# Five pairs of split-weight buffers moved to ten different distances from the stationary tiles in one layer of a hybrid attention / state-space trunk

## The chip, the core and the metric

The kernel runs on one core of one Trainium2 chip. The metric is the device time of one execution in microseconds (us). Start-to-start times of single matmuls are given in nanoseconds (ns).

## What is computed

One layer of a trunk with three groups of heads beside each other, in float32, for 256 tokens of width 4096:

```python
def hybrid_layer(x, norm_w, w_in, w_out, ...):
    h = rms_norm(x, norm_w)
    proj = jnp.einsum('bsd,de->bse', h, w_in)          # 256 x 4096 by 4096 x 14392
    ...                                                # three groups of heads, their gates and norms
    mix = jnp.concatenate([o_fox, o_ssd, o_gdn], axis=-1)
    return x + jnp.einsum('bse,ed->bsd', mix, w_out)   # 256 x 4096 by 4096 x 4096
```

The groups are a forgetting attention (fox), a Mamba-2 scan (ssd) and a gated delta rule (gdn). Nearly all arithmetic lies in the two projections.

## The kernel before

Both projections are worked off in panels of 512 output columns: 28 panels of `w_in` (and 56 gate columns apart), then 8 panels of `w_out`. A panel runs over 32 tiles of the inner dimension (KT = 32). The stationary operand is the activation: for each tile k a buffer `xhl{k}` (later, in the same place, `mhl{k}`) of 128 partitions x 2 x 256 fp32r numbers, the high part and the low part of the same values, 2048 bytes a partition. The moving operand is the weight. SyncE loads two tiles at a time into a buffer `wr` (L226); `split_w` then makes the high part `wh` with a cast on ScalarE (L203) and the low part `wl` with a subtraction on VectorE (L204), each 128 x 512 fp32r, 2048 bytes a partition. `product` issues six matmuls of 512 columns for the tile, for each of the two blocks of 128 tokens (tb):

```python
nc.tensor.matmul(ps[tb], h, wh, start=k == 0, stop=False)           # L214
nc.tensor.matmul(ps[tb], lo, wh, start=False, stop=False)           # L215
nc.tensor.matmul(ps[tb], h, wl, start=False, stop=k == KT - 1)      # L216
```

So `wh` is read four times, `wl` twice, and each matmul has a weight load of its own, of 128 columns of `xhl` (512 bytes a partition).

The pool `wstream` holds four buffers of `wr` and five each of `wh` and `wl`, used in turn. Pools lie in memory in the order in which they are opened. In the built program every `xhl` starts at an address that leaves 128 when divided by 512 (the first at 16512), and so does every half of one, of 512 bytes; the `wh` stand at 98432, 100480, 102528, 104576, 106624 and the `wl` at 108672 to 116864, all of which leave 128 as well. The distance between what a matmul streams and what the next one's weight load reads is thus 0 modulo 512 in all 6,912 of them (36 panels x 32 x 6). The pools behind `wstream` (constants, heads, small tiles) begin at 118912; the heads' tiles leave 32.

The heads' work is cut into generators that `drive` advances by a step after each tile, so that it is strewn between the panels' matmuls. The order of all instructions is set when the program is built. Two more places have matmuls of 512 columns: `gate_chunk` (L243) streams `xhl{k}` past eight stationary tiles of 112 columns, `gw`, which stand 448 bytes apart from a place that leaves 32, and `warm_up` (L154) runs eleven matmuls of zeros at the start.

Of the kernel before, what the change touches and what calls it, by code (L numbers as in the profile page):

```python
# [11 lines left out]
F32R = mybir.dt.float32r  # L12
# [7 lines left out]
P = 128  # L20
# [37 lines left out]
CONV.update({f"sx{_u}": 512 * _u for _u in range(3)}, sB=1536, sC=2048)  # L58
TAPS = 4

C_GN = 0
C_FQ = C_GN + 1
C_FK = C_FQ + 1
# [27 lines left out]
@with_exitstack  # L91
def tile_hybrid(ctx: ExitStack, tc: tile.TileContext, x, xT, w, wo, prm, cst, lev, cvw, out):
    nc = tc.nc

    xp = ctx.enter_context(tc.tile_pool(name="xsplit", bufs=1))
    wp = ctx.enter_context(tc.tile_pool(name="wstream", bufs=5))
    cp = ctx.enter_context(tc.tile_pool(name="const", bufs=1))
    hp = ctx.enter_context(tc.tile_pool(name="heads", bufs=1))
    sp = ctx.enter_context(tc.tile_pool(name="small", bufs=4))
# [98 lines left out]

    def split_w(wr, pinned=False):

        wh = wp.tile([P, 512], F32R, tag="wh", name="wh")
        wl = wp.tile([P, 512], F32R, tag="wl", name="wl")
        a = nc.scalar.copy(wh, wr)  # L203
        b = nc.vector.tensor_tensor(out=wl, in0=wr, in1=wh.bitcast(F32), op=ALU.subtract)  # L204
        if pinned:
            pin(a)
            pin(b)
        return wh, wl
# [12 lines left out]
    def panel(src, lhs):  # L221

        ps = [pp.tile([P, 512], F32, tag="proj", name="proj") for _ in range(2)]
        for c in range(0, KT, CK):
            wr = w_tile()
            nc.sync.dma_start(out=wr, in_=src[:, c:c + CK, :])  # L226
            for j in range(CK):
                wh, wl = split_w(wr[:, j, :])
                product(ps, lhs(c + j), wh, wl, c + j)
                drive()  # L230
        return ps
# [28 lines left out]
    def first_panels(srcs):  # L260
# [24 lines left out]
        for k in range(KT):  # L285
            c, j = k // CK * CK, k % CK
            if j == 0 and 0 < c < KT - CK:
                load(c + CK)
            if k == 8:
                load_consts(xhl[k][:, 0, 0:1].bitcast(F32))  # L290
                clear_past(xhl[k][:, 0, 0:1].bitcast(F32))
            for i in range(len(srcs)):
                wh, wl = split_w(wr[c, i][:, j, :], True)
                product(ps[i], xhl[k], wh, wl, k)
            if k + 1 < KT:
                t, jj, n = xr[k + 1]
                split_x(t, jj, k + 1)
            t, jj, n = xr[k]
            if jj == n - 1:
                square_x(t, n)  # L300
            if (k + 1) % GK_STEP == 0:
                gate_chunk(gp, k + 1 - GK_STEP)
# [195 lines left out]
    def to_mix(src, kt0, ncol, step=0):  # L498

        n = src[0].shape[1]  # L500
        for i0 in range(0, n, 2):
            m = min(2, n - i0)
            ps = bank("mps")
            for i in range(m):
                for tb in range(2):
                    nc.tensor.transpose(ps[:, i * T + tb * P:i * T + tb * P + P], src[tb][:, i0 + i, :], ident)  # L506
            for i in range(m):
                kt = kt0 + i0 + i
                if kt < 12:
                    mt = cp.tile([P, T], F32, name=f"mix{kt}")  # L510
                elif kt < 24:
                    mt = h1([P, T], F32, name=f"mix{kt}")
                else:
                    if kt % 4 == 0:
                        st["fmix"] = r4([P, 4, T], name=f"fmix{kt}", tag="keep")
                    mt = st["fmix"][:, kt % 4, :]
                c = ncol + step * (i0 + i)
                nc.scalar.activation(mt, ps[:, i * T:(i + 1) * T], AF.Copy, scale=prm_s[:, c:c + 1])
                mix[kt] = mt
            yield  # L520

    def gated_norm(ot, c, z):

        for tb in range(2):
            for h in range(HG):
                nc.vector.scalar_tensor_tensor(out=ot[tb][:, h, :], in0=ot[tb][:, h, :],
                                               scalar=c[:, tb * HG + h:tb * HG + h + 1],
                                               in1=z[:, tb, h * P:h * P + P], op0=ALU.mult, op1=ALU.mult)
            yield 2
# [205 lines left out]
    def gdn_out(g, z):  # L735
        yield from gated_norm(gd[g]["ot"], gd[g]["c"], z)
        yield from to_mix(gd[g]["ot"], 4 * g, C_GN)

# [280 lines left out]
    for i in range(8):  # L1019
        cs = slice(i * 512, (i + 1) * 512)  # L1020
        ps = panel(wo[i].rearrange("p (j n) -> p j n", n=512), mix_split)
        for tb in range(2):
# [3 lines left out]
            n = 2 if i == 7 and tb == 1 else 1  # L1026
# [39 lines left out]
def _trace(nc, arrays):  # L1066
    args = {n: nc.dram_tensor(f"in_{n}", v.shape, mybir.dt.from_np(v.dtype), kind="ExternalInput").ap()
            for n, v in arrays.items()}
    args["out"] = nc.dram_tensor("out_0", (T, D), F32, kind="ExternalOutput").ap()
    with tile.TileContext(nc, schedule_with_timeline_sim=True) as tc:  # L1070
        tile_hybrid(tc, **args)
# [11 lines left out]
```

## Time and profile before

| | us |
|---|---|
| median of 2 runs | 1742.24 (1742.17 to 1742.31) |
| the profiled execution | 1739.72 |
| its span, from the first to the last instruction | 1737.9 |
| TensorE busy (matmuls) | 1715.7, 99% |
| weight loads (beside the matmuls) | 1410.1, 81% |
| VectorE busy | 1162.0, 67% |
| ScalarE busy | 933.0, 54% |
| mean granted TensorE clock | 0.999 |

A matmul's own duration is no measure of its cost here: matmuls are pipelined, one of 512 columns is shown with 0.39 us, and the next starts after 0.23 us. What a matmul costs is read from one start to the next. The timeline gives starts to 0.01 us, so that a single step is known to some 10 ns only; over a row of steps the mean is sharper. Where a row stands for several matmuls, its start is that of the first.

### The profile page before, as it was taken

The numbers are of one execution on the slowest core, as the hardware profiler recorded it, in microseconds if no ns is written. First come the engines' busy times: TensorE is split into PE (matmuls) and PEld (weight loads), VectorE is DVE, ScalarE is ACT, GpSimd is POOL, SyncE is SP. The second block draws the span as 40 slices with busy tenths as digits, with TensorE's granted clock in tenths as the row PEclk, the third lists the DMA queues.
The fourth block names the chain that finished last, engine by engine and source line by source line (L and its number), as shares of the span: only waits on it lengthen the run. The fifth ranks groups of instructions, "written<-read, shape, count | busy, mean of one in ns | idle before, by whom it ended". The sixth has DMA issues, their size and how long they took to land.

```text
span 1737.9 us, 24143 instructions
## 1 busy us (share of the span) xinstructions
PE 1715.7 (99%) x8165; PEld 1410.1 (81%) x8165; DVE 1162.0 (67%) x2121; ACT 933.0 (54%) x1635; POOL 89.1 (5%) x73
## 2 busy tenths in 40 slices
PE   9999999998999999999999999999999999999999
PEld 7888878786888778887788888888888888888887
DVE  7668777786676887768776665555755765555554
ACT  6665555445555464546555555556555754444443
POOL 0000020001000020000222100000000000000000
PEclk9999999999999999999999999999999999999999
DMA  8768876665665857667886666665666677777764
GB/s 292 225 216 286 266 233 204 220 200 173 212 224 154 277 163 224 205 199 264 262 274 196 183 186 185 191 202 172 184 194 183 180 243 216 218 217 217 206 205 139
DMA packets 119507, 368.86 MB, mean 212 GB/s; under 512 B 12629, under 2 KB 16045, under 8 KB 119383
## 3 DMA queue, kind: packets, MB, share of 16 engines
q1 hardware_dynamic: 114055, 358.15, 66.4%
q10 hardware_dynamic: 5328, 9.17, 1.5%
q8 instruction: 64, 1.05, 0.2%
q14 instruction: 60, 0.49, 0.1%
HBM read 355.61 MB, written 11.67 MB: 211 GB/s over the span
## 4 chain that ended last, share of the span: by engine, by line
PE 72%; DMA 2%; DVE 1%; issue 1%; ACT 1%; SPq 0%; DVEq 0%; ACTq 0%
PE proj L216 22%; PE proj L214 22%; PE proj L215 22%; DMA tap<-in_cvw 1%; PE yp L809 1%; DVE wl L204 0%; PE kkps L603 0%; PE mps L506 0%; PE zps L581 0%; PE yps L581 0%; PE zqs L581 0%; DMA dmat<-gsum 0%; PE cor L581 0%; ACT L432 0%; PE o L581 0%
## 5 line engine op out<-in xcount | busy, mean ns | idle before, releaser
L204 DVE TENSOR_TENSOR wl<-wr,wh 128x512 fp32r<-128x512 f32 x1152 | 799.0, 708 | 476.9 <-ACT wh L203 420.6
L203 ACT CAST wh<-wr 128x512 fp32r<-128x512 f32 x1152 | 704.8, 621 | 713.8 <-DVE wl L204 304.0
L214 PE MATMUL proj<-wh,xhl 128*128 128x512 f32 x1792 | 707.0, 395 | 9.0 <-ACT wh L203 6.0
L215 PE MATMUL proj<-wh,xhl 128*128 128x512 f32 x1792 | 702.9, 392 | 0.0
L216 PE MATMUL proj<-wl,xhl 128*128 128x512 f32 x1792 | 678.8, 396 | 6.3 <-DVE wl L204 6.0
L214 PEld LDWEIGHTS proj<-wh,xhl 128*128 128x128 f32 x1792 | 337.3, 188 | 81.0 <-ACT wh L203 8.4
L216 PEld LDWEIGHTS proj<-wl,xhl 128*128 128x128 f32 x1792 | 334.9, 188 | 82.2 <-DVE wl L204 14.8
L215 PEld LDWEIGHTS proj<-wh,xhl 128*128 128x128 f32 x1792 | 337.3, 188 | 69.1
L215 PE MATMUL proj<-wh,mhl 128*128 128x512 f32 x512 | 199.4, 390 | 0.0
L214 PE MATMUL proj<-wh,mhl 128*128 128x512 f32 x512 | 199.3, 390 | 0.0
L216 PE MATMUL proj<-wl,mhl 128*128 128x512 f32 x512 | 195.5, 390 | 0.0
L216 PEld LDWEIGHTS proj<-wl,mhl 128*128 128x128 f32 x512 | 96.2, 188 | 19.9
L214 PEld LDWEIGHTS proj<-wh,mhl 128*128 128x128 f32 x512 | 96.1, 188 | 19.9
L215 PEld LDWEIGHTS proj<-wh,mhl 128*128 128x128 f32 x512 | 96.2, 188 | 19.9
L473 DVE TENSOR_TENSOR shift<-shift,tap 128x1024 f32<-128x1024 f32 x42 | 51.3, 1221 | 20.5 <-DMA tap<-in_cvw 20.3
L648 DVE TENSOR_TENSOR tn<-tn,zps 128x512 f16<-128x512 f16 (+1 forms) x36 | 24.5, 682 | 3.5 <-PE zps L581 3.5
L649 DVE TENSOR_TENSOR tt<-tt,zqs 128x512 f16<-128x512 f16 (+1 forms) x36 | 24.5, 680 | 0.0
L793 POOL TENSOR_TENSOR xd<-xtok,spl 128x384 f32<-128x384 f32 (+2 forms) x12 | 16.7, 1398 | 127.5 <-ACT xtok L485 78.2
L430 DVE TENSOR_SCALAR dmat<-dmat,csum 128x128 f32<-128x128 f32 x72 | 16.4, 287 | 9.8 <-DMA dmat<-gsum 9.8
L657 POOL TENSOR_TENSOR res<-cst_s,tn 128x512 f32<-128x512 f32 x6 | 8.2, 1360 | 265.1 <-DVE tn L648 253.4
L639 ACT CAST y<-yps 128x512 f16<-128x512 f32 x36 | 19.3, 586 | 3.9 <-PE yps L581 3.8
L432 ACT ACTIVATE dmat<-dmat 128x384 f32<-128x384 f32 (+1 forms) x22 | 12.2, 554 | 14.5 <-DVE dmat L430 14.3
(302 smaller groups left out, 918.7 us busy)
## 6 DMA issues: line engine op xcount, KB each, us to landing
wr<-in_w SPq DMA_DIRECT2D x446, 512.0 KB, 3.8
wr<-in_wo SPq DMA_DIRECT2D x128, 512.0 KB, 3.6
shift<-past SPq DMA_DIRECT2D x42, 512.0 KB, 5.1
tap<-in_cvw SPq DMA_DIRECT2D x61, 256.0 KB, 6.4
xres<-in_x ACTq DMA_DIRECT2D x16, 256.0 KB, 4.9
xr<-in_xT SPq DMA_DIRECT2D x15, 257.0 KB, 4.9
out<-xres ACTq DMA_DIRECT2D x15, 256.0 KB, 4.2
dmat<-gsum SPq DMA_DIRECT2D x16, 192.0 KB, 6.5
```

The costliest lines, as they stand in the source:

```text
L203: a = nc.scalar.copy(wh, wr)
L204: b = nc.vector.tensor_tensor(out=wl, in0=wr, in1=wh.bitcast(F32), op=ALU.subtract)
L214: nc.tensor.matmul(ps[tb], h, wh, start=k == 0, stop=False)
L215: nc.tensor.matmul(ps[tb], lo, wh, start=False, stop=False)
L216: nc.tensor.matmul(ps[tb], h, wl, start=False, stop=k == KT - 1)
L430: pin(nc.vector.tensor_scalar(out=t[:, i, :], in0=t[:, i, :], scalar1=st["cs"][:, tb, c0 + i:c0 + i + 1], scalar2=0.0, op0=ALU.subtract, o ...
L473: pin(nc.vector.tensor_tensor(out=sh, in0=sh, in1=wj, op=ALU.mult))
L639: nc.scalar.copy(y[tb], v4(ps))
L648: nc.vector.tensor_tensor(out=tn2, in0=tn[tb], in1=v4(zp), op=ALU.subtract)
L649: nc.vector.tensor_tensor(out=tt2, in0=tt[tb], in1=v4(zq), op=ALU.subtract)
L793: nc.gpsimd.tensor_tensor(out=xd[:, o:o + n, :], in0=xv, in1=bc(st["spl"][:, tb, h0:h0 + n], 64), op=ALU.mult)
L809: nc.tensor.matmul(yp[:, h * 64:h * 64 + 64], m[h // 3][:, h % 3, :], xd[:, h, :], start=True, stop=True)
```

## The change

The five turns of `wh` and `wl` become ten buffers with tags of their own, each with a small tail that is never used: 16 elements (64 bytes), or 8 (32 bytes) for `wl3`. The names and the shape that the rest of the kernel sees are as before.

```diff
+SHIFT = {"wh": (4, 4, 4, 4, 4), "wl": (4, 4, 4, 2, 4)}
...
-    wp = ctx.enter_context(tc.tile_pool(name="wstream", bufs=5))
+    wp = ctx.enter_context(tc.tile_pool(name="wstream", bufs=1))
+    turn = [0]
...
     def split_w(wr, pinned=False):
 
-        wh = wp.tile([P, 512], F32R, tag="wh", name="wh")
-        wl = wp.tile([P, 512], F32R, tag="wl", name="wl")
+        i = turn[0]
+        turn[0] = (i + 1) % 5
+        wh, wl = (wp.tile([P, 512 + 4 * SHIFT[n][i]], F32R, tag=f"{n}{i}", name=f"{n}{i}_")[:, 0:512]
+                  for n in ("wh", "wl"))
```

In the built program the buffers now alternate, and their distances from the stationary tiles modulo 512 are:

| turn | 0 | 1 | 2 | 3 | 4 |
|---|---|---|---|---|---|
| wh: address, distance | 98432, 0 | 102656, 128 | 106880, 256 | 111104, 384 | 115296, 480 |
| wl: address, distance | 100544, 64 | 104768, 192 | 108992, 320 | 113216, 448 | 117408, 32 |

All that stands behind the pool moves up by 608 bytes; the heads' tiles then leave 128 modulo 512. No instruction is added, removed or moved: on all five engines the same operations on the same operands stand in the same order, with a wait at the same places, as the two built programs show row by row.

## Rows read from the trace of the kernel before

**Rows 1.** The page: busy time, share, instructions; the granted clock in 40 slices.

```profile
PE 1715.7 (99%) x8165; PEld 1410.1 (81%) x8165; DVE 1162.0 (67%) x2121; ACT 933.0 (54%) x1635; POOL 89.1 (5%) x73
PEclk9999999999999999999999999999999999999999
```

**Rows 2.** The page, costliest groups: busy us, mean ns of one | idle before, its releaser.

```profile
L204 DVE TENSOR_TENSOR wl<-wr,wh 128x512 fp32r<-128x512 f32 x1152 | 799.0, 708 | 476.9 <-ACT wh L203 420.6
L203 ACT CAST wh<-wr 128x512 fp32r<-128x512 f32 x1152 | 704.8, 621 | 713.8 <-DVE wl L204 304.0
L214 PE MATMUL proj<-wh,xhl 128*128 128x512 f32 x1792 | 707.0, 395 | 9.0 <-ACT wh L203 6.0
L214 PEld LDWEIGHTS proj<-wh,xhl 128*128 128x128 f32 x1792 | 337.3, 188 | 81.0 <-ACT wh L203 8.4
L214 PE MATMUL proj<-wh,mhl 128*128 128x512 f32 x512 | 199.3, 390 | 0.0
```

**Rows 3.** Waits of PE: who waited for whom, us in total, times, longest.

```profile
PE proj L216 <- DVE wl L204: 6.0, 12, 1.1
PE proj L214 <- ACT wh L203: 6.0, 2, 4.2
PE proj L214 <- ACT raw_gz L992: 3.0, 2, 2.2
```

**Rows 4.** Groups of PE from 1500 to 1700 us, the output projection.

```profile
L214 PE MATMUL proj<-wh,mhl 128*128 128x512 f32 x295 | 114.9, 389 | 0.0
L215 PE MATMUL proj<-wh,mhl 128*128 128x512 f32 x294 | 114.5, 389 | 0.0
L216 PE MATMUL proj<-wl,mhl 128*128 128x512 f32 x295 | 112.3, 389 | 0.0
```

**Rows 5.** Timeline of PE and PEld, 403 us: start us, us, engine, line, operation.

```profile
402.94 0.40 PE L216 MATMUL proj<-wl,xhl 128*128 128x512 f32 x1
402.94 0.19 PEld L214 LDWEIGHTS proj<-wh,xhl 128*128 128x128 f32 x1
```

**Rows 6.** Timeline of PE, 26.6 to 28.9 us: a chunk of gate columns.

```profile
26.60 0.39 PE L216 MATMUL proj<-wl,xhl 128*128 128x512 f32 x1
26.83 2.02 PE L243 MATMUL gproj<-xhl,gw 128*112 128x512 f32 x8
28.68 0.40 PE L214 MATMUL proj<-wh,xhl 128*128 128x512 f32 x1
```

**Rows 7.** Timeline of PE, 884 to 888 us: behind two matmuls of a head.

```profile
884.10 0.81 PE L827 MATMUL yops<-sst,sC 128*128 128x384 f32 x2
...
884.98 0.39 PE L215 MATMUL proj<-wh,xhl 128*128 128x512 f32 x1
885.21 0.40 PE L216 MATMUL proj<-wl,xhl 128*128 128x512 f32 x1
...
885.68 0.39 PE L215 MATMUL proj<-wh,xhl 128*128 128x512 f32 x1
885.90 0.39 PE L216 MATMUL proj<-wl,xhl 128*128 128x512 f32 x1
...
887.06 0.39 PE L215 MATMUL proj<-wh,xhl 128*128 128x512 f32 x1
```

**Rows 8.** Timeline of PE, 640 to 651 us: two blocks of head matmuls.

```profile
639.77 0.39 PE L214 MATMUL proj<-wh,xhl 128*128 128x512 f32 x1
...
644.08 0.62 PE L581 MATMUL yps<-tn,mb 128*128 128x128 f16 x8
...
644.83 0.40 PE L216 MATMUL proj<-wl,xhl 128*128 128x512 f32 x1
...
646.90 0.39 PE L216 MATMUL proj<-wl,xhl 128*128 128x512 f32 x1
...
649.40 0.40 PE L581 MATMUL zps<-y,tt 128*128 128x128 f16 x4
649.63 0.39 PE L581 MATMUL zqs<-tt,y 128*128 128x128 f16 x4
649.86 0.39 PE L581 MATMUL zps<-y,tt 128*128 128x128 f16 x4
650.08 0.39 PE L581 MATMUL zqs<-tt,y 128*128 128x128 f16 x4
```

## The prediction

> **What bounds the kernel now.** I read the page first, then PE's waits, then the timeline, because only starts tell what a matmul costs here. [...] The two engines that feed TensorE are busy for two thirds and for half of the time, and each idles longest for the other or for free buffers [rows 1, 2]; PE waits for them for some 15 us in all [rows 3]. So the span is the number of matmuls times the distance from one start to the next, and all that the change can do must show in that distance.
>
> The distance in the undisturbed state: from 1500 to 1700 us, 884 matmuls touch the window [rows 4]. A matmul of 0.39 us touches it when it starts between 1499.61 and 1700, so 200.39 us / 884 = 226.7 ns. The same comes out in the input projection: 19 steps from 639.77 to 644.08 us, 226.8 ns [rows 8]. [...] The step is also the same for `wh` and `wl`, for `xhl` and `mhl`.
>
> Beside each matmul runs the weight load of the next, from the same start on [rows 5], for 188 ns [rows 2]. Both read the state buffer, and in this kernel always at places that are equal modulo 512 bytes.
>
> **What the change touches.** It adds no instruction, takes none away and moves none. The casts and subtractions have the same shapes (621 and 708 ns [rows 2]); they write to starts that are multiples of 32 bytes as before, and I cost them at nothing: their engines idle 714 and 477 us in those groups [rows 2], so a rise of a tenth in 799.0 + 704.8 us of work would stay hidden; without that cover, were PE to wait for each, a tenth of 708 ns x 1,152 would be 82 us. The rotation is still five deep. What is left is one thing: in 6,912 matmuls the place of the moving operand against the place of the weight load beside it changes, from always 0 to ten values, four matmuls at one, two at the next, and so on. At one turn in five `wh` stays at 0, though between others.
>
> **What a step costs at other distances.** The trace of before holds no panel matmul at another distance in a steady run, so I bound it from rows near by.
>
> - The gate columns are the nearest: the same 512 moving columns of fp32r, with eight stationary tiles 448 bytes apart, so that the distance changes with every matmul (the loads that run beside them lie at 160, 224, 288, 352, 416, 480, 32 and, for the panel's matmul behind, 0). From 26.83 to 28.68 us are eight steps: 231.3 ns [rows 6]. The load has 112 columns in place of 128. The step just before, in which the distance went from 0 to 96, took 0.23 us, no more than the others.
> - Out of step at distance 0: behind two head matmuls the panel's steps are not 226.7 at once. From 884.98 to 887.06 are nine steps, 231.1 ns in the mean [rows 7]; the two from 885.21 to 885.68 take 235 ns each, the next, to 885.90, 0.22 us. Behind a block of fp16 matmuls it is the same: 644.83 to 646.90, nine steps, 230.0 ns [rows 8]. After nine or ten steps the row is back at 226.7. So the short step is a state into which a row of matmuls settles when nothing disturbs it, and a disturbance costs some 4 ns a step until then.
>
> With the change something is disturbed after every second or fourth matmul: the moving operand's place jumps by 64 bytes, or by 32 at two places of the round. A row that needs nine undisturbed steps to settle gets four at most. I therefore take the unsettled step for all of them, 231.1 ns, between the gate rows' 231.3 and the 230.0 behind fp16 blocks: 231.1 - 226.7 = 4.4 ns more.
>
> **How many pay it.** Some are unsettled now. 8,165 - 6,912 = 1,253 matmuls are not the panels'; in the rows they come in blocks of 2, 8 and 16 [rows 7, 8], 8.7 in the mean, which makes 144 blocks and, with nine steps each, 1,300 unsettled steps; some blocks lie closer than nine steps, so I take 1,200. The sum: (6,912 - 1,200) x 4.4 ns = 25.1 us. On the profiled execution's 1739.72 us (span 1737.9 and 1.8 around it) that gives 1764.8; the runs' median is 2.5 us above that execution, so 1767 for a median, and I say 1766. The waits of [rows 3] may shrink by a few us as TensorE becomes slower, which is why I go down and not up.
>
> **Bounds of the step.** Above: 235 ns, the two dear steps of [rows 7], for all that settle now: 8.3 x 5,712 = 47 us, 1790; for all 6,912, 57 us, 1799. Below: 0.22 us, the short step of [rows 7], some 3 ns below the settled one: 6,912 x 3 = 21 us less, 1721. I stay at 231.1 since two independent kinds of rows give it as a mean, while both ends are single steps that follow one another.
>
> [...] In the trace the gate rows, whose loads wander, are at 231.3 where the panels are at 226.7 [rows 4, 6]. [...]
>
> **Rivals.**
>
> 1. *The place does not matter; nothing happens.* What unsettles a row would be the block of other matmuls, and in the gate columns the shorter load. For it: the first step at distance 96 is as short as the others [rows 6]. Against: the gate rows do not settle over eight steps. Time: 1742.
> [...]
> 3. *The bad distances last.* If a wrong distance holds a row at the dear step rather than at the mean of a swing, the steps are 235: 1790, over 2% more. For it: such steps stand next to each other in [rows 7]. Against: they are followed by a short one.
>
> **How the numbers follow.** The forecast, steps of 229.5 to 233 ns, 1756 to 1778: 0.55. Rival 1: 0.17. Rival 2: 0.13. Rival 3, 1778 to 1799: 0.15. The range for 8 in 10 takes in rival 1, most of rival 3 and a part of rival 2: 1732 to 1796; the forecast's own is 1756 to 1778. 2% of the time is 35 us, about what a measurement of this kernel can tell from no change: 1707 and 1777. Faster by more needs more than half of the distances free: 0.05. Slower by more is rival 3 and the upper edge of the forecast: 0.22. Within 2%: 0.73.
>
> **What would show it.** If right: the window from 1500 to 1700 us, now 884 matmuls, holds 867 or so; the steps vary from buffer to buffer and do not settle to 226.7 anywhere, also where no head works; the casts, subtractions and waits are as before. Wrong, by rival 1: 884 again. [...] By rival 3: about 853, with steps of 235 that come back with the same buffer. Were the casts or subtractions to take longer, or PE's waits in [rows 3] to grow, the cause would lie outside all of this.

## The result, and the profile after

| | before | after |
|---|---|---|
| median, us | 1742.24 | 1764.71 (1763.06 to 1766.37, 2 runs) |
| profiled execution, us | 1739.72 | 1766.37 |
| ratio, 95% interval | | 1.0135 (1.0109 to 1.0162) |

The changed kernel is slower by 1.35% (the two medians alone make 1.29%), less than 2% and clear of the noise. The forecast was 1766.

The page of the changed kernel, its busy times and its clock, which answer to [rows 1]:

```profile
PE 1743.2 (99%) x8165; PEld 1409.9 (80%) x8165; DVE 1162.8 (66%) x2121; ACT 932.5 (53%) x1635; POOL 86.5 (5%) x73
PEclk9999999999999999999999999999999999999999
```

The counts are the same on every engine, VectorE and ScalarE worked as long as before (1162.8 against 1162.0, 932.5 against 933.0 us), and the clock is the full one. Only the matmuls take 27.5 us longer. PE's idle time is 1764.6 - 1743.2 = 21.4 us of the span, against 22.2 before. So nothing waits more; the matmuls follow each other more slowly.

How much more slowly, from the windows of the changed kernel (busy us and instructions of each engine, granted clock, DMA), where the same stretch held 884 matmuls before [rows 4]:

```profile
1500.00:1700.00 200.00, 200.00 (x864) 161.96 (x863) 104.52 (x156) 89.72 (x147) 0.00 (x0) 1.00 0.70 210
```

200.39 us / 864 = 231.9 ns a step, where it was 226.7. No head works in this stretch, so that the row has all the time to settle, and does not. The timeline of the same stretch, PE alone:

```profile
1600.12 0.39 PE L220 MATMUL proj<-wh__15166,mhl 128*128 128x512 f32 x1
1600.35 0.39 PE L221 MATMUL proj<-wl__15167,mhl 128*128 128x512 f32 x1
1600.59 0.39 PE L219 MATMUL proj<-wh__15176,mhl 128*128 128x512 f32 x1
1600.81 0.40 PE L220 MATMUL proj<-wh__15176,mhl 128*128 128x512 f32 x1
1601.05 0.39 PE L221 MATMUL proj<-wl__15177,mhl 128*128 128x512 f32 x1
...
1603.60 0.39 PE L220 MATMUL proj<-wh__15198,mhl 128*128 128x512 f32 x1
1603.83 0.39 PE L221 MATMUL proj<-wl__15199,mhl 128*128 128x512 f32 x1
```

16 steps from 1600.12 to 1603.83 us, 231.9 ns again. The order on PE is also seen here: two matmuls with `wh`, one with `wl`, two, one. The moving operand's place therefore changes after every second and every single matmul, more often than the four and two that the prediction spoke of.

Taken over the whole trace, the 6,534 steps under 260 ns from one panel matmul to the next have a mean of 231.6 ns (before: 227.5); the difference makes 6,534 x 4.1 = 27 us, which is the whole loss of the profiled execution (26.7). Sorted by the buffer that is streamed, the steps to the next start in the output projection run from 229.0 ns at 192 to 234.5 at 64, with 230.8 at 256 and 232.0 at 0. Even the turn at distance 0, whose place is that of before, takes 232.0.

### The profile page after: what moved, and what is told of

Its sections match the earlier page's. It is cut to its first block, busy times and chain, and to the rows that moved or that the text cites. A ratio compares the mean times of both kernels' runs of the same rounds, so it can differ in the third digit from the quotient of the medians.

```text
span 1764.6 us, 24143 instructions
## 1 busy us (share of the span) xinstructions
PE 1743.2 (99%) x8165; PEld 1409.9 (80%) x8165; DVE 1162.8 (66%) x2121; ACT 932.5 (53%) x1635; POOL 86.5 (5%) x73
## 4 chain that ended last, share of the span: by engine, by line
PE 69%; DMA 3%; DVE 2%; issue 1%; ACT 1%; SPq 0%; DVEq 0%; ACTq 0%
PE proj L221 22%; PE proj L219 21%; PE proj L220 21%; DMA tap<-in_cvw 2%; DMA dmat<-gsum 1%; DMA wr<-in_w 1%; PE yp L814 0%; PE kkps L608 0%; PE mps L511 0%; PE zps L586 0%; PE yps L586 0%; PE zqs L586 0%; PE cor L586 0%; DVE raw_sx L479 0%; DVE shift L478 0%
## 5 line engine op out<-in xcount | busy, mean ns | idle before, releaser
L176 DVE SCALAR_TENSOR_TENSOR xhl<-xr,xhl 128x256 fp32r<-128x256 f32 x32 | 15.3, 479 | 3.5 <-ACT xhl L175 3.5
L175 ACT ACTIVATE xhl<-xr 128x256 fp32r<-128x256 f32 x32 | 16.2, 507 | 2.1 <-DMA xr<-in_xT 2.1
L631 DVE TENSOR_TENSOR mb<-m,lev_s 128x512 f16<-128x512 f16 x42 | 16.0, 416 | 0.0
L586 PE MATMUL zps<-y,tt 128*128 128x128 f16 x144 | 14.1, 220 | 1.8 <-ACT y L644 1.8
L586 PEld LDWEIGHTS <-mb 128*128 128x128 f16 x168 | 9.5, 98 | 7.9 <-issue 4.4
L574 POOL TENSOR_TENSOR ktail<-raw_gk,dec 128x512 f32<-128x512 f32 x3 | 3.5, 1168 | 228.9 <-DVE sqn L719 228.9
L586 PEld LDWEIGHTS <-tt 128*128 128x128 f16 x144 | 8.9, 98 | 7.1 <-issue 7.1
L1034 DVE TENSOR_TENSOR xres<-xres,proj 128x512 f32<-128x512 f32 (+1 forms) x17 | 10.4, 650 | 5.4 <-PE proj L221 5.4
L586 PE MATMUL zqs<-tt,y 128*128 128x128 f16 x144 | 13.9, 219 | 0.0
L814 PEld LDWEIGHTS yp<-xd,dmat 128*128 128x128 f32 x96 | 12.7, 191 | 1.1
L814 PE MATMUL yp<-xd,dmat 128*128 128x64 f32 x96 | 12.1, 267 | 0.0
```

The source lines that it names most:

```text
L175: pin(nc.scalar.activation(t[:, 0, :], xr[:, jj, 0:T], AF.Copy, scale=sc))
L586: nc.tensor.matmul(ps[:, h * P:h * P + P], lhs(h), rhs(h), start=True, stop=True)
L814: nc.tensor.matmul(yp[:, h * 64:h * 64 + 64], m[h // 3][:, h % 3, :], xd[:, h, :], start=True, stop=True)
```

## Experiments

Two theories were to be told apart. *Changing costs*: any constant distance settles at 226.7 ns, and only jumps unsettle the row (the prediction's step). *The value costs*: each distance has a step of its own, and 0 happens to be a cheap one. Where a kernel holds one distance through a panel, its buffers are 640 columns wide and a slice of 512 is taken at the wanted place; the mean step of a panel of the output projection is the time from its first to its last start divided by 191. The first of these panels still has matmuls of a head in it; there only its uninterrupted stretches count, from the tenth step on. Runs without a number of executions were executed once. Where an edit starts from the kernel of another run, it is said; `...` in an edit marks lines left out.

### Ten buffers, all at distance 0

```diff
-SHIFT = {"wh": (4, 4, 4, 4, 4), "wl": (4, 4, 4, 2, 4)}
+SHIFT = {"wh": (32, 32, 32, 32, 32), "wl": (32, 32, 32, 32, 32)}
...
```

> The changed kernel with tails of 512 bytes on all ten buffers, so that every distance is 0 again; tags, rotation and the shift of all that stands behind stay of the changed kernel's kind. If the distances are the cause, whether by their values or by their changing: steps of 226.7 ns in the output projection and 1742 us, within 3. If it is something else in the change (ten tags, other addresses of the heads' tiles): about 1764 us, steps of 231 to 232 ns.

Measured: 1738.31 us (10 runs) beside 1737.94 of the kernel before on the same chip, ratio 0.9995 (0.9981 to 1.0009). The windows of this kernel show the 884 of before:

```profile
1500.00:1700.00 200.00, 200.00 (x884) 165.69 (x883) 106.33 (x157) 90.99 (x148) 0.00 (x0) 1.00 0.68 211
```

The tags and the code of the rotation cost nothing. What stands behind the pool moves here by 5,120 bytes, a multiple of 512, and not by 608 as in the change; that its place modulo 512 is not the cause is seen from the output projection of the changed kernel, where no head works and the step is 231.9 ns all the same. It is the distances.

### One distance through a whole panel

```diff
...
-        wh = wp.tile([P, 512], F32R, tag="wh", name="wh")
-        wl = wp.tile([P, 512], F32R, tag="wl", name="wl")
+        dh, dl = place()      # by panel: 0, 64, 128, ... in the output projection
+        wh = wp.tile([P, 640], F32R, tag="wh", name="wh")[:, dh // 4:dh // 4 + 512]
+        wl = wp.tile([P, 640], F32R, tag="wl", name="wl")[:, dl // 4:dl // 4 + 512]
```

> Both buffers at one distance through a whole panel (192 matmuls), another one in the next: 0, 64, 128, 192, 256, 320, 384, 448 in the eight panels of the output projection, 26 further values in the input projection. If a change of distance unsettles a row and any constant distance settles: 226.7 ns a step in every panel after some ten matmuls, 43.5 us a panel of the output projection, 1742 to 1745 us in all. If each distance has a step of its own and 0 is a cheap one: 226.7 ns at 0 alone, 229 to 235 at the others (44.0 to 45.1 us a panel), 1764 to 1790 us. [...]

Measured: 1765.11 us, as much as the changed kernel, with a single change of distance per panel. The timeline of this kernel, the first and the last matmul of six panels (distances 64, 128, 192, 256, 320, 384):

```profile
1448.97 0.40 PE L225 MATMUL proj<-wh,mhl 128*128 128x512 f32 x1
...
1492.70 0.39 PE L227 MATMUL proj<-wl,mhl 128*128 128x512 f32 x1
1492.93 0.40 PE L225 MATMUL proj<-wh,mhl 128*128 128x512 f32 x1
...
1537.32 0.40 PE L227 MATMUL proj<-wl,mhl 128*128 128x512 f32 x1
1537.56 0.40 PE L225 MATMUL proj<-wh,mhl 128*128 128x512 f32 x1
...
1582.13 0.39 PE L227 MATMUL proj<-wl,mhl 128*128 128x512 f32 x1
1582.36 0.39 PE L225 MATMUL proj<-wh,mhl 128*128 128x512 f32 x1
...
1625.67 0.39 PE L227 MATMUL proj<-wl,mhl 128*128 128x512 f32 x1
1625.90 0.40 PE L225 MATMUL proj<-wh,mhl 128*128 128x512 f32 x1
...
1669.63 0.39 PE L227 MATMUL proj<-wl,mhl 128*128 128x512 f32 x1
1669.86 0.40 PE L225 MATMUL proj<-wh,mhl 128*128 128x512 f32 x1
...
1714.26 0.40 PE L227 MATMUL proj<-wl,mhl 128*128 128x512 f32 x1
```

| distance | 0 | 64 | 128 | 192 | 256 | 320 | 384 | 448 |
|---|---|---|---|---|---|---|---|---|
| step, ns | 226.7 | 229.0 | 232.4 | 233.4 | 226.8 | 229.0 | 232.4 | 233.4 |

For 64: (1492.70 - 1448.97) / 191 = 229.0 ns. A constant distance need not settle at 226.7. It settles, but into a short cycle of steps: 226, 229 or 230, 231 or 232 at 64; 233, 233, 234 at 192. And what counts repeats after 256 bytes, not 512: 64 and 320, 128 and 384, 192 and 448 agree to 0.1 ns. That falls to *the value costs*.

The two other distances of the change stand in the input projection of the same run, at 32 and at 480:

```profile
130.06 0.40 PE L225 MATMUL proj<-wh,xhl 128*128 128x512 f32 x1
...
134.49 0.39 PE L226 MATMUL proj<-wh,xhl 128*128 128x512 f32 x1
...
465.23 0.40 PE L225 MATMUL proj<-wh,xhl 128*128 128x512 f32 x1
...
470.13 0.40 PE L226 MATMUL proj<-wh,xhl 128*128 128x512 f32 x1
```

19 steps of 233.2 ns and 21 of 233.3.

The distance alone does not fix the cycle, however. The panel at 496 has one break, eight matmuls of a head:

```profile
1308.55 0.39 PE L225 MATMUL proj<-wh,xhl 128*128 128x512 f32 x1
...
1325.55 0.40 PE L225 MATMUL proj<-wh,xhl 128*128 128x512 f32 x1
1325.79 1.04 PE L904 MATMUL fps<-cst_s,raw_fk 128*128 128x128 f32 x8
...
1326.89 0.40 PE L227 MATMUL proj<-wl,xhl 128*128 128x512 f32 x1
...
1353.87 0.40 PE L227 MATMUL proj<-wl,xhl 128*128 128x512 f32 x1
```

75 steps of 226.7 ns ahead of it, 114 of 236.7 behind it, at the same distance. So a distance can hold a row in more than one cycle, and a disturbance can take it from one to another. What picks the cycle was not tested.

### The low part alone

Against the kernel with one distance a panel:

```diff
         p = cur["p"]
-        d = 0 if p < 0 else INNER[p] if p < 26 else OUTER[p - 26]
-        return d, d
+        return 0, (0 if p < 0 else INNER[p] if p < 26 else OUTER[p - 26])
```

> wh stays at distance 0, wl alone is moved, by another amount in each panel (0, 64, 128, ... 448 in the output projection), so that two matmuls at 0 and one at the other distance follow each other. If changing is what costs: all steps dear, 230 to 232 ns in the mean in every panel but the one at 0, about 1764 us. If the value costs: a third of the steps dear, 228.3 ns in the mean, about 1751 us.

Measured: 1758.61 us, between the two. Windows of this kernel, inside the panels with `wl` at 64, 128, 256 and 384:

```profile
1445.00:1485.00 40.00, 40.00 (x174) 32.37 (x174) 19.71 (x29) 18.02 (x30) 0.00 (x0) 1.00 0.68 217
1489.00:1529.00 40.00, 40.00 (x174) 32.27 (x173) 19.58 (x30) 17.70 (x29) 0.00 (x0) 1.00 0.68 218
1578.00:1618.00 40.00, 40.00 (x178) 33.10 (x177) 19.94 (x30) 18.40 (x30) 0.00 (x0) 1.00 0.68 220
1666.00:1706.00 40.00, 40.00 (x175) 32.50 (x174) 20.09 (x30) 18.09 (x30) 0.00 (x0) 1.00 0.65 207
```

174 matmuls in 40.39 us are some 232 ns, 178 are 227. With `wl` at 64 the panel's mean is 231.8 ns, far over (2 x 226.7 + 229.0) / 3 = 227.5, which the values alone would give, and over the step of either distance; at 256 it is 226.9, although the place changes as often. So a change inside a tile costs too, here 4.3 ns a step, but not one by 256. The agreement of distances 256 apart does not hold throughout: with `wl` at 128 the panel's mean is 232.7 ns, at 384 231.1.

### A change after every n tiles

Against the kernel with one distance a panel:

```diff
+EVERY = (8, 4, 1, 2, 4, 8, 16, 0)
...
-        p = cur["p"]
-        d = 0 if p < 0 else INNER[p] if p < 26 else OUTER[p - 26]
+        p, k = cur["p"], cur["k"]
+        cur["k"] = k + 1
+        d = 0 if p < 0 or EVERY[p % 8] == 0 else 64 * (k // EVERY[p % 8]) % 512
         return d, d
```

> Both buffers at one distance that moves by 64 bytes after every n tiles (6 n matmuls); the panels of the output projection have n = 1, 2, 4, 8, 16, never, 8, 4. If a change unsettles some nine steps at 231 ns and the row then settles at 226.7: 231, 230, 228.3, 227.5, 227.1, 226.7, 227.5, 228.3 ns in the mean of these panels. If the value costs: about the same 230 to 233 ns for every n, and 226.7 in the panel without change alone.

Measured: 1754.27 us. Panels of the output projection, against the mean of the constant steps of the same distances (230.4 ns for all eight, as for 0 to 192; 227.8 for 0 and 64):

| n | 1 | 2 | 4 | 8 | 16 | never |
|---|---|---|---|---|---|---|
| step, ns | 231.6 | 231.4 | 230.8 | 230.5 | 228.0 | 226.9 |
| by the values | 230.4 | 230.4 | 230.4 | 230.4 | 227.8 | 226.7 |

Windows of this kernel inside the panels with n = 2, 8 and 16:

```profile
1442.00:1482.00 40.00, 40.00 (x175) 32.47 (x174) 20.05 (x30) 18.41 (x30) 0.00 (x0) 1.00 0.65 212
1530.00:1570.00 40.00, 40.00 (x176) 32.59 (x175) 19.72 (x30) 17.87 (x30) 0.00 (x0) 1.00 0.68 221
1574.00:1614.00 40.00, 40.00 (x177) 32.98 (x176) 19.94 (x30) 18.17 (x30) 0.00 (x0) 1.00 0.68 221
```

Most of what lies over 226.7 is the values; what comes on top shrinks with n, from 1.2 ns at n = 1 to 0.1 at n = 8, some 5 to 12 ns for each change (6 x 1.2, 12 x 1.0, 24 x 0.4, 48 x 0.1). These changes come between tiles, by 64 bytes and for both buffers at once; the changed kernel also changes inside each tile, as the low part alone does. Neither theory alone gives this row: at n = 8 changing alone would be 227.5, and the values alone know no n.

### The stationary tiles moved instead

```diff
+    gp0 = ctx.enter_context(tc.tile_pool(name="gap0", bufs=1))
+    gp0.tile([P, 16], F32, name="gap0")
     xp = ctx.enter_context(tc.tile_pool(name="xsplit", bufs=1))
+    gp1 = ctx.enter_context(tc.tile_pool(name="gap1", bufs=1))
+    gp1.tile([P, 112], F32, name="gap1")
```

> wh and wl stay where they were (they leave 128 modulo 512), the stationary tiles move up by 64 bytes instead, so that the distance is -64, that is 448, in all 6,912 matmuls. If the distance between the two counts: the step of 448 in the run with one distance a panel, 233.4 ns in a cycle of 233, 233, 234; 6.7 ns more on some 6,540 steps, 1738 + 44 = 1782 us. If the place of the moving buffers by itself counts: 226.7 ns, 1738 us. If only a changing distance costs: 226.7 ns and 1738 us as well.

Measured: 1772.36 us (4 runs), ratio 1.0196 (1.0179 to 1.0213). The windows of this kernel:

```profile
1500.00:1700.00 200.00, 200.00 (x859) 161.15 (x858) 102.58 (x153) 87.81 (x143) 0.00 (x0) 1.00 0.66 209
```

200.39 / 859 = 233.3 ns, the step of distance 448, with the moving buffers where they always were; the run with one distance a panel had moved those and left the stationary tiles. It is the distance between the two operands and not the place of one of them, and a distance that never changes is enough for a loss of 33.5 us. The 44 that were expected counted from 226.7 ns; from the mean of before, 227.5, the sum is 6,540 x 5.8 = 38; some of it came back in the gaps over 260 ns between panel matmuls, which fell from 88.3 to 83.4 us.

### More distances

The kernel with one distance a panel, other numbers in its lists.

> One distance a panel as before, 34 others: 60, 124, 188, 248, 12, 104, 120, 200 in the output projection, multiples of 4 up to 244 in the input projection. If the step is a matter of where the moving stream meets the weight load within 256 bytes: 226 to 237 ns, each value near its neighbours (60 near 229, 124 near 232, 188 near 233, 248 between 236 and 227), none under 226.7, about 1764 us. [...]

Measured: 1769.35 us; no panel under 226.7 ns. As short as 0 are 28, 60 and 156 (226.7 each); 12 has 228.9, 124 and 188 have 230.0, 200 has 233.3, 120 has 234.3, 244 has 239.8 and 116 has 240.0. Neighbours are not alike: 120 lies 4 bytes from either of 116 and 124. Over both runs with one distance a panel 57 of the 64 multiples of 4 modulo 256 were held; 226.7 ns was the step at 0, 28, 60, 156 and 252, and in part of a panel at 240 (the 496 above). A second value at one distance is seen here too: the panel at 196 has 240.0 ns ahead of its head matmuls and 233.3 behind them. At 116 the steps are all equal, in the timeline of this kernel:

```profile
742.22 0.40 PE L225 MATMUL proj<-wh,xhl 128*128 128x512 f32 x1
...
744.86 0.40 PE L227 MATMUL proj<-wl,xhl 128*128 128x512 f32 x1
```

11 steps, 240.0 ns each.

### High and low part woven together

The loads of `xhl` and `mhl` now read every second element: one of 128 columns spans 1024 bytes in place of 512 and takes some 194 ns (33.34 us of loads in 40 us, at a step of 233.3 ns, in the first window below), where it took 188 [rows 2].

Against the kernel with one distance a panel:

```diff
-        return xp.tile([P, 2, T], F32R, tag=f"xhl{k}", name=f"{name}{k}")
+        return xp.tile([P, T, 2], F32R, tag=f"xhl{k}", name=f"{name}{k}").rearrange("p t a -> p a t")
...
```

> High and low part of a stationary tile lie interleaved, so that a weight load of 128 columns reads every second number of 1024 bytes and runs through memory twice as fast; one distance a panel, 0, 64, 128, ... 448 in the output projection. [...]

Measured: 1767.8 us (one run). The panels at 64, 128, 192 and 256 have 233.3, 231.4, 230.05 and 233.3 ns, those from 320 to 448 233.3, 231.4 and 230.05 again: a period of 256 once more in these panels, other values, and none under 226.7. Windows of this kernel, at 64 and at 448:

```profile
1452.00:1492.00 40.00, 40.00 (x173) 33.34 (x172) 19.65 (x30) 17.71 (x29) 0.00 (x0) 1.00 0.68 216
1719.00:1759.00 40.00, 40.00 (x176) 33.78 (x175) 19.19 (x28) 16.76 (x27) 0.00 (x0) 1.00 0.50 157
```

Distance 64 goes from 229.0 to 233.3 ns (173 matmuls in 40.39 us), so the layout of the loads does matter. The stride is not the only thing that it changes: the low part now starts 4 bytes behind the high part, so that their loads stand at two distances. That a load at this pace and the stream miss each other for good at some distances, the author's guess behind this run, is not borne out: no panel came under 226.7 ns, the step at 0 in the plain layout.

### Cheap distances mixed

Again a change after every matmul tile, this time between places that are cheap when constant, and between dear ones.

```diff
...
+        of = (0,) if p < 26 else OUTER[p - 26]
+        return of[k % len(of)], of[k % len(of)]
```

> The input projection at distance 0; in the output projection the distance of both buffers changes after every tile (six matmuls), among distances whose own constant step was short or long: panels with 0/256, 0/28, 0/60, 0/156, 0/252, 28/60/156/252 (all 226.7 to 226.8 when constant), 448/192 (both 233.4) and 128/448 (232.4 and 233.4). If the value alone counts: 226.7 ns in the first six panels, 233.4 and 232.9 in the last two. If a change costs by itself: 0/256 at 226.7 (the same place modulo 256), the next five at 229 to 232 ns, the last two not under 233.

Measured: 1740.4 us (the kernel before beside it 1736.4).

| places | 0, 256 | 0, 28 | 0, 60 | 0, 156 | 0, 252 | 28, 60, 156, 252 | 448, 192 | 128, 448 |
|---|---|---|---|---|---|---|---|---|
| step, ns | 226.7 | 228.9 | 228.9 | 226.8 | 227.9 | 227.9 | 233.3 | 233.1 |

(0, 252 without two gaps of 451 and 334 ns.)

Windows of this kernel inside the panels with 0 and 28, 0 and 156, 448 and 192:

```profile
1427.00:1467.00 40.00, 40.00 (x177) 32.75 (x176) 20.38 (x31) 17.88 (x30) 0.00 (x0) 1.00 0.69 221
1515.00:1555.00 40.00, 40.00 (x178) 33.06 (x177) 20.12 (x30) 18.16 (x30) 0.00 (x0) 1.00 0.68 221
1647.00:1687.00 40.00, 40.00 (x173) 32.24 (x172) 20.08 (x29) 18.01 (x30) 0.00 (x0) 1.00 0.65 206
```

Changing costs between nothing (0 and 156) and 2.2 ns a step (0 and 28), by the pair; a change to another place of the same value (448 and 192, 256 apart) costs nothing at the dear value too. Where the place changes between tiles only, the value is the larger part.

### Fewer loaded columns

All distances at 0; in the output projection all tiles but the first and the last of a panel load n of their 128 columns, and the product is added up in n partitions only: the other partitions of the result lack these terms.

```diff
-            h, lo = (t[:, i, tb * P:tb * P + P] for i in range(2))
+            n = P if k in (0, KT - 1) else COLS[0]
+            h, lo = (t[:, i, tb * P:tb * P + n] for i in range(2))
...
```

> All distances 0. In the output projection the matmuls of tiles 1 to 30 of a panel load only n of the 128 stationary columns and leave the other rows of the result without these terms: n = 128, 112, 96, 80, 64, 48, 32, 128 in the eight panels; the stream of 512 columns stays. [...]

Measured: 1745.19 us (the kernel before beside it 1736.4).

| columns loaded | 128 | 112 | 96 | 80 | 64 | 48 | 32 |
|---|---|---|---|---|---|---|---|
| step, ns | 226.7 | 229.0 | 229.9 | 233.1 | 229.9 | 235.1 | 231.6 |

The windows of PE alone (its busy us and matmuls, clock, DMA) of this kernel, with 64, 48 and 128 columns, and one of its groups of weight loads from the stretch with 48:

```profile
1564.00:1604.00 40.00, 40.00 (x176) 1.00 0.68 220
1608.00:1648.00 40.00, 40.00 (x172) 1.00 0.64 202
1697.00:1737.00 40.00, 40.00 (x178) 1.00 0.50 157
```

```profile
L217 PEld LDWEIGHTS proj<-wh,mhl 128*48 128x48 f32 x50 | 6.1, 122 | 5.6
```

The load becomes shorter, 188 ns at 128 columns [rows 2] and 122 at 48, and the step longer, 226.7 ns and 235.1. A loss in proportion to what the load reads would have made the step shorter as the columns became fewer, and one that the columns have no part in would have left it at 226.7; neither is seen. The shape of the load changes the step as another distance does, by no order that these seven values show. It also tells that the gate rows' 231.3 ns [rows 6] were bad witnesses: their loads had 112 columns, and 112 columns at distance 0 alone make 229.0.

### A dear and a cheap distance everywhere

Against the kernel with one distance a panel:

```diff
-        p = cur["p"]
-        d = 0 if p < 0 else INNER[p] if p < 26 else OUTER[p - 26]
-        return d, d
+        return 116, 116
```

> All ten buffers at distance 116 in the whole kernel, the dearest constant distance seen (240.0 ns in its panel). If the value of the distance is what costs: 240 ns in every panel, 12.5 ns over the 227.5 that the kernel before has in the mean, on some 6,540 steps: 82 us less what shorter waits give back (the kernel with 448 stayed 5 us under this sum), 1737 + 77 = 1814 us. If only changes of distance cost: 1737.

Measured: 1799.09 us (4 runs), ratio 1.0350 (1.0333 to 1.0367). The windows of this kernel:

```profile
1500.00:1700.00 200.00, 200.00 (x847) 158.65 (x846) 101.22 (x149) 86.58 (x142) 0.00 (x0) 1.00 0.65 203
```

200.39 / 847 = 236.6 ns here, where the input projection has stretches at 236.7 and others at 240.0: one distance in more than one cycle again. The direction is that of *the value costs*, the size 60 us in place of 77: the mean step of the trace is 237.9 and not 240, and the gaps over 260 ns fall from 88 to 74 us.

The same with 156 in both places:

> All ten buffers at distance 156, which is no multiple of 64 and as far from 0 as most, but had 226.7 ns when constant. If the value of the distance is what costs: 226.7 ns, 1737 us, the same as before within 3. If 0 (and 256) alone are cheap as a place in memory: 1760 or more.

Measured: 1735.65 us (10 runs), ratio 0.9985 (0.9976 to 0.9994), the shortest time of all the kernels here, and by 0.15% only. The windows of this kernel show 883 matmuls where 884 stood [rows 4]:

```profile
1500.00:1700.00 200.00, 200.00 (x883) 164.77 (x882) 106.35 (x157) 89.82 (x148) 0.00 (x0) 1.00 0.67 212
```

The settled step is thus no shorter. What differs is the way there. The timeline of this kernel behind the head block that [rows 7] show in the kernel before (line 827 there, 835 here):

```profile
880.37 0.81 PE L835 MATMUL yops<-sst,sC 128*128 128x384 f32 x2
...
881.24 0.39 PE L221 MATMUL proj<-wh,xhl 128*128 128x512 f32 x1
...
882.16 0.39 PE L222 MATMUL proj<-wl,xhl 128*128 128x512 f32 x1
...
883.97 0.39 PE L221 MATMUL proj<-wh,xhl 128*128 128x512 f32 x1
```

Four steps of 230 ns, then eight of 226.3: settled after four, where nine were needed before. That is one place. Over the whole trace 386 panel steps lie between 229 and 260 ns, where 941 did before, and the mean step is 227.0 ns for 227.5, which makes some 3 us: the size of the gain, which is itself barely clear of the noise.

## Why the prediction was right

**What bounds the kernel.** Right: the span is the number of matmuls times their distance. PE waits no more than before, the casts and subtractions took as long as before, and the loss of the profiled execution is that of the steps. Nothing settled to 226.7, as it had said.

**The sum.** Forecast 231.1 ns a step and 867 matmuls between 1500 and 1700 us; measured 231.6 over the trace, 231.9 in that stretch and 864 matmuls. Forecast 25.1 us; measured 26.7 in the profiled execution and 22.5 between the medians. The term of 1,200 steps that were unsettled already, 1,200 x 4.4 = 5.3 us, holds: the 6,530 steps of before lie 0.8 ns over the settled one in the mean, 5.2 us.

**The step that failed in its reason** is "a state into which a row of matmuls settles when nothing disturbs it", with the 226.7 ns that it ascribed to any undisturbed row. A row does settle, but its distance decides at what: 226.7 at 0, 28, 60, 156 and 252 modulo 256, up to 240.0 elsewhere, and at some distances at one of two values. At a constant 448, with no change of distance at all, the whole kernel stood at 233.3 (1772.36 us), where this step would have had it at 226.7 and 1738.

How much of the change's own loss is value and how much is changing stays open. For the values: the constant steps of its distances have a mean of 230.3 ns for `wh` (0, 128, 256, 384, 480) and 231.6 for `wl` (64, 192, 320, 448, 32), two to one 230.7, which is 4.0 of the 4.9 ns from 226.7 to 231.6. Against reading that as four fifths: sorted by buffer, the steps of the changed kernel do not follow these values (192 has 233.4 when constant and is its shortest at 229.0; 0 has 226.7 and takes 232.0), and in each turn of the change `wl` stands 64 bytes beyond `wh`; held at 64 and 0 through a panel, in the same order of matmuls, they make 231.8 where the values make 227.5. A run that changes inside each tile between cheap distances would tell the two apart; there is none.

So the size is in part luck. The 231.1 ns of a row on its way back to 226.7 stood in for a state that is not on its way anywhere, and lies near the mean of these ten distances as well. For other sets the same working fails: five turns between 0 and 256 would have been forecast at 231, and as the panel with 0 and 256 shows they settle at 226.7.

**Rival 1**, that the place does not matter, falls with the stationary tiles moved by 64 bytes: 33.5 us by a distance that never changes.

**Rival 2**, that some distances are free and the kernel becomes faster: the chances given to it, and the part of the range that reaches down to 1732 us for it, rest on an estimate of the author's that no run shows. No distance held constant in any run gave a panel under 226.7 ns, the step at 0, and in the changed kernel no buffer's steps are shorter than 229.0 ns in the mean.

**Rival 3**, that a bad distance holds the row at a dear step, is what the kernels with a constant distance do; its 235 ns were too high for these ten distances (226.7 to 233.4) and not for others (116, 244). In the changed kernel its sign, steps of 235 that come back with the same buffer, is seen at 64 alone (234.5), a distance that is not dear when constant.

**Open.** What lies behind it, in the state buffer or on TensorE's side, was not settled. It depends on the distance modulo 256 (226.7 to 240.0 ns), on the layout and the number of the loaded columns (233.3 ns woven where 229.0 plain, at 64; 235.1 with 48 columns where 226.7 with 128), and on what came before: the steps just ahead (up to 4.3 ns between 0 and 64) and the state in which a row was left (226.7 or 236.7 at 496). It is not in proportion to what is loaded (229.9 ns with 64 columns, 235.1 with 48, 231.6 with 32). A stream with no weight load beside it was not tried.

## What to carry to other kernels

Where fp32r matmuls of 512 columns follow each other with a weight load beside each, the distance between the streamed buffer and the stationary tile belongs to the kernel's tuning: here it was worth up to 3.5%, and a padding of 64 bytes ahead of one pool (with 448 behind it) cost 2%. Keep both operands at equal places modulo 256 bytes (226.7 and 226.8 ns a step here, at 0 and 256) unless a measured distance is better, and look at the offsets again after any change to a pool ahead of them. Read such an effect from the starts of matmuls or their count in a window. A single duration in the timeline hides it (0.39 or 0.40 us at every distance shown here); the mean over a group hints at it, 389 ns before [rows 4] and 398 with all distances at 116, in the same window.

## What was not expected of the hardware

- The period is 256 bytes where the distance is constant: eight distances from 0 to 448 agree in pairs to 0.1 ns in the plain layout, and three of the pairs again in the woven one. Where 0 takes turns with another distance it need not hold (232.7 ns with 128, 231.1 with 384).
- The means that come back most stand 3.3 ns apart, at a granted clock of 1.00: 226.7, 230.0, 233.3, 236.7 and 240.0 ns. Some are rows of equal steps (116), some short cycles of steps (228 and 232 at 124), as the values between are (226, 229 or 230, 231 or 232 at 64).
- Neighbours 4 bytes apart differ by up to 10 ns (226.7 at 0 and 236.7 at 4; 240.0 at 116, 234.3 at 120, 230.0 at 124), and one distance can have two values in one panel, ahead of and behind eight matmuls of a head (496: 226.7, then 236.7; 196: 240.0, then 233.3).
- Loading fewer columns lengthened the step, to 235.1 ns at 48.
